# Rounding a transposed bank in two blocks of four instead of turn by turn, in a two-layer attention trunk on one Trainium2 core

## The chip, the cores and the metric

The kernel runs on one core of one Trainium2 chip. The core's engines are TensorE (PE, with its weight loads PEld), VectorE (DVE), ScalarE (ACT), GpSimd (POOL) and SyncE (SP, which issues most transfers); each works through its own list of instructions in order and waits for others by semaphores. The metric is device microseconds of one execution.

## The reference

Two layers, each `x + mixer(rms_norm(x))`, on 256 tokens of width 1024. Layer 0 is a sparse-attention mixer with 16 query heads and 4 key and value heads: compressed keys, selected blocks and a window, joined by gates. Layer 1 is a sliding-window mixer with attention sinks.

```python
def reference(x, positions, norm_gains, a_w_in, ..., b_w_in, ..., b_w_out, ...):
    for i in range(DEPTH):                      # DEPTH = 2
        h = rms_norm(x, norm_gains[i])
        y = nsa_mixer(h, ...) if i == 0 else swa_sink_mixer(h, ...)
        x = x + y
    return x

def nsa_mixer(h, ...):
    q, kc, vc, ks, vs, kw, vw, gl, z = jnp.split(h @ w_in, ...)
    ...                                         # rope, norms, three attentions, gates
    return (o.reshape(b, s, MIX_WIDTH) * jax.nn.silu(z)) @ w_out
```

## The kernel before

All arithmetic is float32. For TensorE every operand is split into a high part, rounded to the chip's fast float32 form, and a low part, the remainder; a product is three matmuls (high by high, high by low, low by high). For a weight block, a raw tile `wraw` comes by DMA (SP issues it when one of 5 raw buffers is free), ScalarE copies it to `wh` (L147; one by GpSimd in the opening), VectorE subtracts to `wl` (L175, "the weight split"). In the opening the blocks are 128x512 (two), 128x1024, 128x912 and 128x608 elements.

The 256 rows are two halves of 128. `norm_transpose` (L262 to L279) makes the transposed rows `hT` of a half, high and low: for each of two groups of four 128x128 blocks, four transposes on TensorE (L269) fill one PSUM bank `ptn`; then for each k ScalarE rounds block k times the gain to the high part (L275, "the rounding") and VectorE makes the low part from the bank and the high part (L278). There are two such banks, which serve other transposes too. A layer has four groups, so eight groups in the program; layer 0 takes the first group of both halves, some keep-warm matmuls, then the second group, and layer 1 takes the halves one after the other.

The projections of the opening of layer 0 are, in TensorE's order, `akc` (compressed keys and values, 48 matmuls of 512 columns), `avw` (window values and gates, 48 of 304), `akw` (window keys, 24 of 256), with `ptc` (16 transposes of the compressed part) among them, then `aks`. Later come `aq` (queries), `pz` (the z gate), the scores `s`, the softmax on VectorE (`cwide` L740, `p` L411), ScalarE and GpSimd, the attention `po`, and the output projections `pya`, `pyb`, which also open layer 1 (`aqb`, `akv`).

The order on each engine is not the order of the code. A scheduler with a model of times plans the whole program and places each instruction by priority (`norm_transpose` has its own offsets, 1000 in layer 0 and 200 in layer 1) and by when its inputs are due. So one edit can move rows anywhere behind it. Between instructions on different engines it sets semaphores.

Of the kernel before, what the change touches and what calls it, by code (L numbers as in the profile page):

```python
# [90 lines left out]
def tile_hybrid_trunk(ctx: ExitStack, tc: tile.TileContext, x, positions, norm_gains, a_w_in, a_cmp_pos,  # L91
# [122 lines left out]
    gT = const.tile([128, 16], F32, name="gT")  # L214
# [47 lines left out]
    def norm_transpose(xt, layer, hT, h, ns=(0, 1)):  # L262

        for n in ns:
            pt = ps_t.tile([128, 4, 128], F32, name="ptn", tag="pt")
            for k in range(4):
                nc.tensor.transpose(pt[:, k], xt[:, (4 * n + k) * 128:(4 * n + k + 1) * 128], ident)  # L269
            for k in range(4):  # L270
                kk = 4 * n + k
                gk = gT[:, 8 * layer + kk:8 * layer + kk + 1]
                hi = hT[:, 0, kk, h * 128:(h + 1) * 128]
                if GE[kk % len(GE)] == 'a':
                    nc.scalar.activation(hi, pt[:, k], AF.Copy, scale=gk)  # L275
                else:
                    nc.vector.tensor_scalar(hi, pt[:, k], gk, None, op0=ALU.mult)
                nc.vector.scalar_tensor_tensor(hT[:, 1, kk, h * 128:(h + 1) * 128], pt[:, k], gk, hi.bitcast(F32),  # L278
                                               op0=ALU.mult, op1=ALU.subtract)  # L279

# [211 lines left out]
    hT = work.tile([128, 2, 8, T], F32R, name="hT", tag="hT", bufs=1)  # L492
# [5 lines left out]
    with tc.high_priority(offset=1000):  # L498
        for n in range(2):
            for h in range(2):  # L500
                norm_transpose(xh[h], 0, hT, h, (n,))
                if n == 0 and h == 1:
                    keep_warm(NWARM2)
# [293 lines left out]
    hT = work.tile([128, 2, 8, T], F32R, name="hT1", tag="hT", bufs=1)  # L797
    with tc.high_priority(offset=200):
        for h in range(2):
            norm_transpose(xh[h], 1, hT, h)  # L800
# [107 lines left out]
```

## Time and profile before

| what | value |
|---|---|
| time, median of 3 runs | 289.93 us (288.51 to 290.54) |
| profiled execution | 287.7 us |
| its span, first to last instruction | 285.8 us |
| TensorE busy | 272.5 us, 95% |
| VectorE busy | 210.8 us, 74% |
| ScalarE busy | 194.8 us, 68% |
| GpSimd busy | 129.8 us, 45% |
| granted TensorE clock | 1.00 |

The span leaves 1.9 us of the profiled execution outside. "Busy" sums the time of an engine's instructions; the chain that ended last lies on TensorE for 75% of the span, on VectorE for 9%, on ScalarE for 6%.

### The profile page before, as it was taken

To read this page: it belongs to the slowest core of one execution; us is meant where nothing else is said; L and a number is where in the kernel's file an instruction comes from. 1 tells how busy PE (TensorE), PEld (TensorE's weight loads), DVE (VectorE), ACT (ScalarE), POOL (GpSimd) and SP (SyncE) were. 2 spreads that over 40 slices of the span, in tenths; PEclk is the share of its full clock that TensorE was granted. 3 is DMA by queue.
4 is the path that set the end of the run, shared out by engine and by line. 5 is a ranking of instruction groups with operands and counts; after the bars stand their busy time and mean duration, and the time that the engine had idled before them with its cause. 6 is when DMAs were issued, how large, how long until landed. Compare 5 with 4: busy or idle time off the path is not lost.

```text
span 285.8 us, 5305 instructions
## 1 busy us (share of the span) xinstructions
PE 272.5 (95%) x1780; PEld 228.7 (80%) x1780; DVE 210.8 (74%) x554; ACT 194.8 (68%) x466; POOL 129.8 (45%) x204
## 2 busy tenths in 40 slices
PE   6999999999999997888999999999999999999994
PEld 5857988887988996567767877779988999777774
DVE  3797757759876999857887456388987999986433
ACT  4982885577775857798979367178666787895510
POOL 8893325474630488465353320041495495513200
PEclk9999999999999999999999999999999999999999
DMA  7986955546465365200202427043696453000003
GB/s 227 337 242 229 361 155 144 145 144 172 124 160 168 116 204 165 76 0 0 77 1 73 150 74 221 0 146 85 197 292 169 145 163 133 1 2 0 0 2 147
DMA packets 33402, 37.51 MB, mean 131 GB/s; under 512 B 1968, under 2 KB 21856, under 8 KB 33248
## 3 DMA queue, kind: packets, MB, share of 16 engines
q1 hardware_dynamic: 32960, 37.16, 42.9%
q8 instruction: 14, 0.23, 0.3%
q14 instruction: 12, 0.10, 0.1%
q10 hardware_dynamic: 416, 0.02, 0.1%
HBM read 36.13 MB, written 1.05 MB: 130 GB/s over the span
## 4 chain that ended last, share of the span: by engine, by line
PE 75%; DVE 9%; ACT 6%; POOL 4%; issue 3%; DMA 1%; SPq 0%; ACTq 0%
PE pz L114 8%; PE po L114 8%; PE aqb L114 8%; PE pya L114 8%; PE aq L114 7%; PE pyb L114 6%; PE ptp L444 5%; PE aks L114 4%; PE s L114 3%; PE avw L114 2%; PE sb L114 2%; DVE wl L175 2%; PE akv L114 2%; ACT wh L147 2%; PE pza L114 2%
## 5 line engine op out<-in xcount | busy, mean ns | idle before, releaser
L175 DVE TENSOR_TENSOR wl<-wraw,wh 128x1024 fp32r<-128x1024 f32 (+2 forms) x64 | 81.7, 1281 | 25.0 <-ACT wh L147 24.9
L147 ACT ACTIVATE wh<-wraw 128x1024 fp32r<-128x1024 f32 (+3 forms) x63 | 65.0, 1033 | 29.7 <-PE pya L114 9.7
L71 POOL TENSOR_SCALAR p<-p,rg 128x128 f32<-128x128 f32 (+1 forms) x64 | 27.6, 451 | 26.8 <-DVE rg L767 9.1
L114 PE MATMUL pz<-hT,wh 128*128 128x256 f32 x192 | 36.6, 286 | 0.0
L413 ACT ACTIVATE p<-p,nm 128x128 f32<-128x128 f32 (+1 forms) x64 | 28.5, 448 | 5.7 <-DVE nm L411 5.5
L66 POOL TENSOR_TENSOR rt<-rt,rt 128x512 f32<-128x512 f32 (+2 forms) x14 | 19.1, 1375 | 28.3 <-DVE rt L319 16.7
L114 PEld LDWEIGHTS pz<-hT,wh 128*128 128x128 f32 x192 | 30.5, 191 | 0.3 <-DVE kt L699 0.2
L114 PE MATMUL pz<-hT,wl 128*128 128x256 f32 x96 | 27.4, 285 | 0.0
L411 DVE CUSTOM_DVE_ANT_0 p<-s,mask,nrq 128x128 f32<-128x128 f32 (+1 forms) x64 | 24.5, 409 | 2.3 <-PE ptp L444 2.2
L147 ACT ACTIVATE ptsb<-ptp 128x512 f32<-128x512 f32 x36 | 20.6, 590 | 6.0 <-PE ptp L444 5.9
L114 PE MATMUL s<-kt,qT 128*128 128x272 f32 (+1 forms) x96 | 19.7, 307 | 1.6 <-DVE cwide L740 1.4
L114 PE MATMUL aqb<-wh,hT 128*128 128x512 f32 x64 | 21.0, 397 | 0.0
L114 PE MATMUL aq<-wh,hT 128*128 128x512 f32 x64 | 20.6, 393 | 0.0
L71 POOL TENSOR_SCALAR pb<-pb,rg 128x128 f32<-128x128 f32 (+1 forms) x24 | 11.9, 515 | 16.7 <-DVE rg L864 13.4
L444 PE MATMUL ptp<-identr,p 128*128 128x128 f32 x96 | 16.3, 279 | 2.4 <-ACT ptsb L147 1.3
L114 PEld LDWEIGHTS pz<-hT,wl 128*128 128x128 f32 x96 | 18.3, 191 | 0.0
L114 PEld LDWEIGHTS s<-kt,qT 128*128 128x128 f32 x96 | 14.5, 189 | 3.4 <-PE s L114 1.2
L444 PEld LDWEIGHTS ptp<-identr,p 128*128 128x128 f32 x96 | 11.3, 140 | 5.5 <-ACT ptsb L147 2.0
L413 ACT ACTIVATE pb<-pb,nm 128x128 f32<-128x128 f32 (+1 forms) x32 | 14.2, 447 | 1.3 <-DVE nm L411 1.2
L275 ACT ACTIVATE hT<-ptn,gT 128x128 fp32r<-128x128 f32 x32 | 10.9, 363 | 5.8 <-DVE hT L278 3.4
L411 DVE CUSTOM_DVE_ANT_0 pb<-sb,mask,nsink 128x128 f32<-128x128 f32 (+1 forms) x32 | 13.8, 471 | 0.8 <-PE sb L114 0.6
L114 PEld LDWEIGHTS aq<-wh,hT 128*128 128x128 f32 x64 | 11.9, 188 | 2.2
(249 smaller groups left out, 727.5 us busy)
## 6 DMA issues: line engine op xcount, KB each, us to landing
wraw<-in_a_w_in_dram SPq DMA_DIRECT2D x25, 512.0 KB, 4.3
wraw<-in_b_w_in_dram SPq DMA_DIRECT2D x18, 512.0 KB, 4.0
wraw<-in_a_w_out_dram SPq DMA_DIRECT2D x8, 512.0 KB, 3.6
wraw<-in_b_w_out_dram SPq DMA_DIRECT2D x8, 512.0 KB, 3.6
x<-in_x_dram SPq DMA_DIRECT2D x4, 256.0 KB, 4.1
w<-in_cmp_w_dram SPq DMA_DIRECT2D x1, 1024.0 KB, 4.8
x<-in_x_dram SPq DMA_DIRECT2D x2, 512.0 KB, 3.7
wraw<-in_a_w_in_dram SPq DMA_DIRECT2D x2, 456.0 KB, 5.2
```

Of the source, the lines that this page charges most:

```text
L66: self.eng.tensor_tensor(out, a, b, op=op)
L71: self.eng.tensor_scalar(out, a, s0, s1, op0=op0, op1=op1)
L114: nc.tensor.matmul(o, lhsT=l, rhs=r, start=start, stop=stop)
L147: nc.scalar.activation(dst, src, AF.Copy)
L175: e_.tensor_tensor(wl[:, ks], raw[:, ks], wh[:, ks].bitcast(F32), op=ALU.subtract)
L275: nc.scalar.activation(hi, pt[:, k], AF.Copy, scale=gk)
L411: nc.vector.tensor_tensor_reduce(out=p, in0=s, in1=mk, scale=nr, scalar=floor, op0=ALU.add, op1=ALU.min, accum_out=nm)
L413: nc.scalar.activation(p, p, AF.Exp, scale=-1.0, bias=nm, accum_out=total)
L444: nc.tensor.transpose(pt[:, i], s, ident)
```

## The change

The loop over the four blocks of a bank is cut in two. All four roundings are written first, then all four low parts. Nothing is added or taken away.

```diff
                     nc.scalar.activation(hi, pt[:, k], AF.Copy, scale=gk)
                 else:
                     nc.vector.tensor_scalar(hi, pt[:, k], gk, None, op0=ALU.mult)
+
+            for k in range(4):
+                kk = 4 * n + k
+                gk = gT[:, 8 * layer + kk:8 * layer + kk + 1]
+                hi = hT[:, 0, kk, h * 128:(h + 1) * 128]
                 nc.vector.scalar_tensor_tensor(hT[:, 1, kk, h * 128:(h + 1) * 128], pt[:, k], gk, hi.bitcast(F32),
                                                op0=ALU.mult, op1=ALU.subtract)
```

The low part is on L283 after the change, and lines behind it are 5 further down. Before, ScalarE's rounding of a block waits for the low part of the block before it and each low part for its rounding. After, only the first rounding of a bank waits, and the first low part waits for the fourth rounding. ScalarE's order changes in the same way as VectorE's below: four roundings in a row, then the weights' high parts. SP's order is the same. The scheduler places rows anew on the other engines through most of the program.

VectorE, from the third bank of layer 0 to the split of the first avw weights (`wl` 128x912), before:

```order
L278 SCALAR_TENSOR_TENSOR hT<-ptn,gT,hT 128x128 x2
L175 TENSOR_TENSOR wl<-wraw,wh 128x1024
L278 SCALAR_TENSOR_TENSOR hT<-ptn,gT,hT 128x128
L175 TENSOR_TENSOR wl<-wraw,wh 128x1024
L278 SCALAR_TENSOR_TENSOR hT<-ptn,gT,hT 128x128
L517 TENSOR_SCALAR r0h<-r_129 128x2
L554 TENSOR_SCALAR trig_194<-trig,r_129 128x96 x2
L278 SCALAR_TENSOR_TENSOR hT<-ptn,gT,hT 128x128
L175 TENSOR_TENSOR wl<-wraw,wh 128x1024
L278 SCALAR_TENSOR_TENSOR hT<-ptn,gT,hT 128x128
L175 TENSOR_TENSOR wl<-wraw,wh 128x1024
L278 SCALAR_TENSOR_TENSOR hT<-ptn,gT,hT 128x128
```

The same place after:

```order
L283 SCALAR_TENSOR_TENSOR hT<-ptn,gT,hT 128x128 x4
L175 TENSOR_TENSOR wl<-wraw,wh 128x1024
L283 SCALAR_TENSOR_TENSOR hT<-ptn,gT,hT 128x128 x4
L522 TENSOR_SCALAR r0h<-r_129 128x2
L559 TENSOR_SCALAR trig_194<-trig,r_129 128x96 x2
L175 TENSOR_TENSOR wl<-wraw,wh 128x1024
L608 COPY ktv_211<-pp 128x16
L175 TENSOR_TENSOR wl<-wraw,wh 128x1024 x2
L608 COPY ktv_212<-pp 128x16
L175 TENSOR_TENSOR wl<-wraw,wh 128x912
```

The low parts, spread mostly singly between weight splits before, now stand in fours ahead of the later splits; the two small copies have moved ahead of the 912 split.

TensorE, where avw (both accumulators, 479 and 480) begins, before:

```order
L114 MATMUL akc_215<-wl,hT 128x512
L114 MATMUL akc_216<-wh,hT 128x512
L114 MATMUL avw_479<-wh,hT 128x304
L114 MATMUL avw_480<-wh,hT 128x304
L114 MATMUL akc_216<-wh,hT 128x512
L114 MATMUL akc_216<-wl,hT 128x512
L114 MATMUL akc_215<-wh,hT 128x512 x2
L114 MATMUL akc_215<-wl,hT 128x512
L114 MATMUL avw_479<-wl,hT 128x304
```

After:

```order
L114 MATMUL akc_216<-wl,hT 128x512
L114 MATMUL akc_216<-wh,hT 128x512 x2
L114 MATMUL akc_216<-wl,hT 128x512
L114 MATMUL akc_216<-wh,hT 128x512
L114 MATMUL avw_479<-wh,hT 128x304
L114 MATMUL avw_480<-wh,hT 128x304
L114 MATMUL avw_479<-wl,hT 128x304
```

Before, avw and the last akc matmuls alternate, with the last akc far into avw; after, all 48 akc matmuls stand ahead of the first avw.

TensorE, at the first scores of the second query group (`s1_1097`) among the z matmuls (`pz_1333`), before, with the numbers of the tiles:

```order
L114 MATMUL pz_1333<-hT_128,wl_1337 128x256
L114 MATMUL pz_1333<-hT_128,wh_1336 128x256 x2
L114 MATMUL s1_1097<-kt_198,qT1_205 128x272 x2
L114 MATMUL pz_1333<-hT_128,wl_1337 128x256
L114 MATMUL pz_1333<-hT_128,wh_1336 128x256 x2
```

After:

```order
L114 MATMUL pz_1333<-hT_128,wl_1367 128x256
L114 MATMUL pz_1333<-hT_128,wh_1366 128x256 x2
L114 MATMUL s1_1097<-kt_198,qT1_205 128x272 x2
L114 MATMUL pz_1333<-hT_128,wl_1367 128x256
L114 MATMUL pz_1333<-hT_128,wh_1366 128x256 x2
L114 MATMUL pz_1333<-hT_128,wl_1367 128x256
```

Before, 20 matmuls of `pz_1333` stand ahead of these scores, all with the first weight block (1336); after, 44 do, most of the second block (1366) among them. In layer 1 the first scores (`sb_2670`) stand behind 30 z matmuls instead of 17.

## Rows read from the trace of the kernel before

**Rows 1.** The page, busy time, share of the span and instructions of each engine.

```profile
PE 272.5 (95%) x1780; PEld 228.7 (80%) x1780; DVE 210.8 (74%) x554; ACT 194.8 (68%) x466; POOL 129.8 (45%) x204
```

**Rows 2.** Windows: stretch in us; its length; busy us by engine; PEclk; DMA; GB/s.

```profile
8.60:31.60 23.00, 21.92 (x108) 16.70 (x108) 19.13 (x35) 15.25 (x30) 15.94 (x23) 1.00 0.86 271
31.60:110.00 78.40, 78.02 (x550) 69.95 (x550) 60.05 (x120) 56.27 (x108) 38.17 (x34) 1.00 0.56 168
110.00:175.00 65.00, 60.45 (x391) 46.35 (x390) 45.67 (x200) 48.77 (x150) 27.60 (x65) 1.00 0.23 70
...
240.00:286.00 46.00, 41.39 (x269) 32.66 (x267) 28.45 (x87) 24.36 (x73) 9.88 (x20) 1.00 0.07 25
```

**Rows 3.** The low part's line, L278: who waited for it (us, times).

```profile
  ACT hT L275: 3.4, 8
  PEld akc L114: 2.4, 4
  PE akc L114: 0.8, 2
```

**Rows 4.** ScalarE's timeline: start us, duration us, engine, line, operation, count, idle before.

```profile
6.44 0.37 ACT L275 ACTIVATE hT<-ptn,gT 128x128 fp32r<-128x128 f32 x1 [1.35 <-PE ptn L269]
6.71 0.62 ACT L147 ACTIVATE wh<-wraw 128x512 fp32r<-128x512 f32 x1
...
8.87 1.05 ACT L147 ACTIVATE wh<-wraw 128x1024 fp32r<-128x1024 f32 x1
...
10.07 0.63 ACT L512 ACTIVATE x<-x 128x512 f32<-128x512 f32 x1
...
11.67 1.28 ACT L549 ACT_TABLE_LOAD   x1
```

**Rows 5.** VectorE's timeline in the opening.

```profile
7.36 0.69 DVE L175 TENSOR_TENSOR wl<-wraw,wh 128x512 fp32r<-128x512 f32 x1 [0.17 <-ACT wh L147]
7.97 0.60 DVE L278 SCALAR_TENSOR_TENSOR hT<-ptn,gT,hT 128x128 fp32r<-128x128 f32 x2
...
13.78 2.14 DVE L175 TENSOR_TENSOR wl<-wraw,wh 128x1024 fp32r<-128x1024 f32 x1
...
16.11 1.21 DVE L175 TENSOR_TENSOR wl<-wraw,wh 128x1024 fp32r<-128x1024 f32 x1
...
17.57 0.72 DVE L554 TENSOR_SCALAR trig<-trig,r 128x96 f32<-128x96 f32 x2
...
18.48 1.53 DVE L175 TENSOR_TENSOR wl<-wraw,wh 128x1024 fp32r<-128x1024 f32 x1
...
20.20 1.49 DVE L175 TENSOR_TENSOR wl<-wraw,wh 128x1024 fp32r<-128x1024 f32 x1
...
21.88 1.37 DVE L175 TENSOR_TENSOR wl<-wraw,wh 128x912 fp32r<-128x912 f32 x1
```

**Rows 6.** GpSimd's timeline: the last of the rope tables.

```profile
22.24 1.60 POOL L559 TENSOR_TENSOR tabs<-sm,trig 128x256 f32<-128x256 f32 x1
```

**Rows 7.** TensorE's timeline in the opening.

```profile
8.62 1.20 PE L114 MATMUL akc<-wh,hT 128*128 128x512 f32 x2
...
28.67 0.41 PE L114 MATMUL avw<-wh,hT 128*128 128x304 f32 x1
...
31.71 0.28 PE L114 MATMUL akw<-wh,hT 128*128 128x256 f32 x1
...
33.38 1.03 PE L615 MATMUL ptc<-identr,kd 128*128 128x128 f32 x8
34.17 0.48 PE L114 MATMUL akw<-wh,hT 128*128 128x256 f32 x2
...
35.45 0.40 PE L114 MATMUL aks<-wh,hT 128*128 128x512 f32 x1
```

**Rows 8.** Timelines of VectorE and TensorE in layer 1.

```profile
180.26 0.41 DVE L423 TENSOR_TENSOR oz<-of,oz 128x256 fp32r<-128x256 f32 x1
...
181.41 0.39 PE L114 MATMUL pya<-wh,oz 128*128 128x512 f32 x1
```

## The prediction, made before the changed kernel ran

> **What bounds the kernel now.** I read the page's busy shares first, then the windows by stage, then the line of the low part with who waited for it, and last the three engines' timelines of the first 36 us. TensorE is busy 272.5 of 285.8 us [rows 1], so a gain exists only where it stands idle. The windows [rows 2] say where: from 31.6 to 110 us it works 78.02 of 78.40 us, a wall in which nothing can be won but through which a lead is carried; in the opening, 8.6 to 31.6 us, it is idle 23.00 - 21.92 = 1.08 us; from 110 to 175 us 4.55 us, from 240 us to the end 4.61 us. The granted clock is 1.00 in each of them.
>
> The line of the low part [rows 3] says what the turn-by-turn order costs. ScalarE waited 3.4 us in 8 places for a low part before its next rounding; TensorE waited 2.4 + 0.8 = 3.2 us (weight loads and matmuls together), every time in akc, the first projection of layer 0. No other work of TensorE waited for a low part. So layer 1 holds no wait of TensorE that the change can remove. The 3.2 us of waits are more than the 1.08 us of idle time, since a late weight load is partly covered by the matmul running before it.
>
> **Part by part: the opening.** The change adds and removes no instruction; it makes four roundings of a bank (ScalarE) and four low parts (VectorE) two blocks. What follows is the scheduler's new order around them, and the forecast is the new place of TensorE after it. I take a state that both orders pass: akc 48 matmuls done, avw 46, akw 24 and the transposes ptc 16.
>
> *Before* reaches it thus [rows 7]: the first aks matmul starts at 35.45; akc, avw (48) and akw are done, but only 8 ptc. Eight ptc took 34.17 - 33.38 = 0.79, two avw take 2 x 0.145 = 0.29 (21 avw start between 28.67 and 31.71, 0.145 each). 35.45 + 0.79 - 0.29 = 35.95 us.
>
> *After*, ScalarE starts at 6.44 as before. Neighbours overlap: the next start is about 0.1 before the end of the one before (6.44 + 0.37 against 6.71) [rows 4]. Four roundings: 3 x 0.27 + 0.37 = 1.18, to 7.62. VectorE's four low parts, 0.26 apart (two took 0.60 [rows 5]), run 7.65 to 8.75. The first weight split of 512 (0.69) so ends at 9.3 instead of 7.36 + 0.69 = 8.05. Second bank: roundings 8.0 to 9.2, low parts to 10.3, split to 10.9, the 1024 split to 12.0. ScalarE meanwhile makes a wh of 512 and of 1024 (1.05) and two squares (about 0.63 each), so the third bank's roundings run 11.7 to 12.9, the table load (1.28, 11.67 before) 12.8 to 14.1, the fourth bank 14.3 to 15.45. VectorE: third low parts 12.9 to 13.95, the next weight split from 13.9.
>
> From here VectorE's splits set the end, and their price is not one number. The cheapest 1024 split took 1.21 us (16.11), the three others beside GpSimd's tables 1.49 to 2.14 [rows 5]. I price each by the row nearest in time: the split at 13.9 as the one at 13.78 (2.14), to 16.0; fourth low parts to 17.05; the two trig products (0.72) with the tiny r0h ahead, 0.75, to 17.8; then 1.53 (18.48), 1.53 again and 1.49 (20.20), each less the 0.07 of overlap, and two short copies of 0.1: 17.8 + 3 x 1.45 + 0.2 = 22.35; then the first 912 split as at 21.88 (1.37). It ends at **23.75**. Before, this split stood earlier in the row, between single low parts, and ended at 21.88 + 1.37 = 23.25.
>
> TensorE: akc's 48 start at 8.62 as before, because the keep-warm matmuls ahead of them do not change. Twice as wide as akw (0.119 each, below), one takes 0.24, all of them 11.4; eight transposes take 0.8, and with the first split's lateness the end lies at about 21.3, where akc's own last split (19.3) is long done. The waits for low parts are gone. In their place comes one new wait: avw now stands wholly behind akc and waits for the first 912 split, from 21.3 to 23.8. Behind it on TensorE stands everything else. From 23.80 the state takes 44 avw x 0.145 + 24 akw x 0.119 (14 of them from 31.71 to 33.38) + 16 ptc (2 x 0.79) = 6.38 + 2.86 + 1.58 = 10.82, so 34.62. Gain 35.95 - 34.62 = **1.3 us**.
>
> Bounds of this term: with every split at the 1.21 price the 912 split ends at 22.0 and the gain is 3.1; with every split at 2.14 (912 in proportion, 1.9) it ends at 26.1 and 1.0 us is lost. The gain ends when the split ends at 35.95 - 10.82 - 0.05 = 25.1. I take the middle, since the tables run until 22.24 + 1.60 = 23.84 [rows 6] and, with the table load 1.1 us later, a little longer.
>
> **Layer 1.** No wait on TensorE [rows 3], so nothing to win. What could be lost: oz and of (the gated attention of the second row half) now stand behind all eight low parts instead of six. Before, the last of the three ended at 180.26 + 0.41 = 180.67, and the matmul that reads it started at 181.41 [rows 8]. Two more low parts ahead are 2 x 0.26 = 0.52, which fits the 0.74 of slack, and the low parts take no turns with ScalarE any more. I take 0; bounds: 0 below, 0.5 above, if the cover of TensorE's aqb matmuls there were gone.
>
> **Transfers.** The same loads stand in the same order on SP. A load goes when a raw buffer comes free, with the weight split: the first split lies 1.25 us later, the one at 13.9 as before. Their readers come later too. I take 0.
>
> **Sum.** 287.7 (the profiled run) - 1.3 = 286.4. That run lies 2.2 under the median of the three runs, 289.93; on the median's scale the forecast is 289.93 - 1.3 = **288.6 us**. The wall after 31.6 us carries the lead to 110 us; behind it I assume the same idle time as before.
>
> **The rivals**, on the median's scale.
>
> *R1, the lead grows.* The whole program is planned anew, and 9.2 us of idle time lie behind the wall [rows 2]. If the new order gives back a quarter (2.3), the time is 289.93 - 1.3 - 2.3 = 286.3. For: VectorE starts ropes and sums of the queries earlier. Against: nothing in the change aims at these stages.
>
> *R2, VectorE's splits stay slow.* All at 2.14: 289.93 + 1.0 = 290.9. For: the slow rows lie beside GpSimd's tables. Against: the split at 16.11 took 1.21 [rows 5] with the tables under way until 23.84 [rows 6]. It decides from a first 912 split later than 25.1. The Trainium skill, "SBUF — State Buffer", section "Who interferes with whom", says that VectorE and GpSimd share a port pair under an exclusive lock, which would make the 2.14 the normal price there. The row at 16.11 shows it is not paid each time.
>
> *R3, slower: scores too late.* In the new order the first scores of the second query group, s1_1097, stand behind 44 z matmuls instead of 20, and in layer 1 the first scores behind 30 instead of 17. A z matmul is as wide as akw, 0.119 each: 24 x 0.119 = 2.9 and 13 x 0.119 = 1.6. If the softmax chain of the 110 to 175 us stage hangs on them fully, the time is 289.93 - 1.3 + 2.9 + 1.6 = 293.1; with layer 0 alone 291.5. For: that stage already idles 4.55 us. Against: before it VectorE has other work that the plan moved ahead. It decides when the delay exceeds the 1.3 of lead.
>
> *R4, a coarser grain.* The first split of weights ends 1.25 us later (9.3 for 8.05), because it stands behind four low parts and not one. If that delay runs through the whole opening, it takes back the 1.3: 289.9. For: what stands on VectorE is served in order. Against: TensorE does not start akc before 8.62 [rows 7], and the next splits are late by less. [...]
>
> **How the numbers follow.** A measurement of this kernel tells about 1%, 2.9 us, from no change: faster is below 287.0, slower above 292.8. Forecast 0.45 (own range 286.8 to 290.9, from the split prices; 0.05 of it under 287.0), R1 0.22 (0.19 under 287.0), R2 0.07 (with late scores 0.01 above 292.8), R3 0.20 (0.16 above 292.8, since a late score usually moves more than itself), R4 0.06. Faster 0.24, slower 0.17, same 0.59. Range: down to R1 with the cheaper splits by half, 285.4; up to R3 at its full price, 293.0. About 1 in 10 is left out on each side.
>
> **What would show it.** Right: no wait of akc for a low part; one wait of avw of 2 to 3 us for the first 912 split, which ends at 23 to 24.5; the first aks matmuls about 1.3 us earlier for the same work done; 31 to 110 us still full; layer 1's pya without a wait for oz. Wrong: a 912 split after 25.1 (R2); more than 4.55 us idle between 110 and 175 us, ended by VectorE's cwide or p (R3); or less there and behind 240 us (R1).

## The result

The changed kernel took 286.12 us (median of 4 runs, 285.36 to 286.77) and the kernel before 289.34 us beside it (288.51 to 290.54): a ratio of 0.989, with a 95% interval of 0.9855 to 0.9924. A second comparison gave 0.9902 (0.9868 to 0.9936). The gain is about 1%, or 3 us. One run of the kernel before, of 304.76 us at a mean clock of 0.855, is left out of every comparison. The profiled execution took 285.62 us, against 287.7 before, and its span is 283.8 us, against 285.8.

The page's busy times, which answer to [rows 1]:

```profile
PE 270.9 (95%) x1780; PEld 230.1 (81%) x1780; DVE 208.0 (73%) x554; ACT 194.2 (68%) x466; POOL 128.3 (45%) x204
```

The windows of the kernel after, as in [rows 2] (length, busy us of PE, PEld, DVE, ACT and POOL, PEclk, DMA share, GB/s):

```profile
8.60:31.60 23.00, 21.05 (x119) 17.89 (x118) 19.95 (x37) 16.18 (x33) 17.24 (x24) 1.00 0.81 264
31.60:110.00 78.40, 78.12 (x546) 70.07 (x544) 59.35 (x120) 56.34 (x105) 36.92 (x36) 1.00 0.60 174
110.00:175.00 65.00, 61.32 (x393) 47.62 (x395) 45.82 (x198) 49.74 (x157) 27.79 (x62) 0.97 0.24 73
```

The low part's line, now L283, with who waited for it, as in [rows 3]:

```profile
  PEld pp L607: 0.4, 1
```

No akc matmul waits for a low part any more; one small weight load waits 0.4 us. ScalarE's 3.4 us of waits are gone too. The opening window has not become fuller for it: TensorE's busy time there is 21.05 us, 0.87 less than before, because a new wait stands in it. VectorE's timeline in the opening, as in [rows 5]:

```profile
14.23 1.24 DVE L175 TENSOR_TENSOR wl<-wraw,wh 128x1024 fp32r<-128x1024 f32 x1
...
16.84 1.31 DVE L522 TENSOR_SCALAR r0h<-r 128x2 f32<-128x2 f32 x1
...
18.42 1.21 DVE L175 TENSOR_TENSOR wl<-wraw,wh 128x1024 fp32r<-128x1024 f32 x1
...
19.64 3.36 DVE L175 TENSOR_TENSOR wl<-wraw,wh 128x1024 fp32r<-128x1024 f32 x2
...
23.00 1.54 DVE L175 TENSOR_TENSOR wl<-wraw,wh 128x912 fp32r<-128x912 f32 x1
```

TensorE's timeline, as in [rows 7], from the first akc to the state of the prediction's sum:

```profile
8.92 1.20 PE L114 MATMUL akc<-wh,hT 128*128 128x512 f32 x2
...
22.21 0.44 PE L114 MATMUL avw<-wh,hT 128*128 128x304 f32 x2
24.60 0.41 PE L114 MATMUL avw<-wl,hT 128*128 128x304 f32 x1 [1.95 <-DVE wl L175]
...
35.03 0.60 PE L620 MATMUL ptc<-identr,kd 128*128 128x128 f32 x4
35.38 0.36 PE L114 MATMUL akw<-wh,hT 128*128 128x256 f32 x1
```

VectorE's weight splits (L175) run until the first 912 split ends at 23.00 + 1.54 = 24.54 us, and avw's first low-part matmul starts at 24.60 after an idle wait of 1.95 us. The state of the prediction's sum (akc 48, avw 46, akw 24, ptc 16) is reached at 35.38, against 35.95 before: a lead of 0.57 us, not 1.3. (In all there are 48 akw matmuls, not 24; in both orders the first 24 of them stand ahead of this state, so the comparison is of the same work.)

The rest of the 2.0 us lies elsewhere. Two more places in the program are the same in both orders and can be set beside each other: the first transposes of layer 1 (ptn), and the end.

| | before | after | lead |
|---|---|---|---|
| state in the opening | 35.95 | 35.38 | 0.57 |
| first ptn of layer 1 | 174.94 | 173.27 | 1.67 |
| end of the span | 285.8 | 283.8 | 2.0 |

The two ptn rows, before and after:

```profile
174.94 0.60 PE L269 MATMUL ptn<-identr,x 128*128 128x128 f32 x4
```

```profile
173.27 0.60 PE L269 MATMUL ptn<-identr,x 128*128 128x128 f32 x4
```

Between the opening and layer 1 the lead grows by 1.10 us, in layer 1 by 0.33. The first of these two is found near 70 us. Before, 16 transposes of the selected keys (ptk) stand in one piece (TensorE, start, duration, count):

```profile
69.49 0.70 PE L380 MATMUL ptk<-identr,kp 128*128 128x128 f32 x6
...
70.30 0.36 PE L380 MATMUL ptk<-identr,kp 128*128 128x128 f32 x2
71.02 1.04 PE L380 MATMUL ptk<-identr,kp 128*128 128x128 f32 x8 [0.35 <-ACT kt L381]
72.08 0.50 PE L114 MATMUL pz<-hT,wh 128*128 128x256 f32 x2
```

They share two PSUM banks with ScalarE's copies out of them, and a group of four has to wait until a bank has been copied. The waits of that stretch before the change:

```profile
PEld ptk L380 <- ACT kt L381: 0.5, 1, 0.5
...
PE ptk L380 <- ACT kt L381: 0.4, 1, 0.4
...
PEld pz L114 <- DVE kt L699: 0.2, 1, 0.2
```

After the change the new plan puts the groups apart, among the z matmuls:

```profile
69.52 0.28 PE L114 MATMUL pz<-hT,wl 128*128 128x256 f32 x1
69.64 0.45 PE L385 MATMUL ptk<-identr,kp 128*128 128x128 f32 x4
69.94 0.35 PE L114 MATMUL pz<-hT,wh 128*128 128x256 f32 x1
70.12 0.46 PE L385 MATMUL ptk<-identr,kp 128*128 128x128 f32 x4
```

Four ptk take 69.94 - 69.64 = 0.30 us there; the other eight follow at 73.61. Before, the piece from 69.49 to 72.08 took 2.59 us for 16 ptk and one ptkc (another small transpose, about 0.2): 16 at that pace are 1.2, so that about 1.2 us went in waiting, enough for the 1.10.

The stage of the scores and the softmax is as long as before. Its window in the kernel before, up to the first ptn of layer 1, with 475 matmuls and 474 weight loads:

```profile
100.00:175.00 75.00, 70.45 (x475) 56.35 (x474) 55.46 (x221) 55.08 (x163) 36.51 (x71) 1.00 0.29 88
```

The window of the kernel after with the same 475 and 474, up to its first ptn:

```profile
98.33:173.27 74.94, 71.29 (x475) 57.39 (x474) 56.36 (x226) 56.14 (x168) 36.09 (x71) 0.98 0.28 88
```

75.00 us before, 74.94 after. The granted clock (the column before the last two) is not the same in it. From 110 to 120 us, before and after:

```profile
110.00:120.00 10.00, 7.47 (x48) 5.48 (x46) 8.56 (x41) 7.92 (x29) 4.52 (x10) 1.00 0.39 113
```

```profile
110.00:120.00 10.00, 8.02 (x44) 5.88 (x44) 8.84 (x42) 7.55 (x30) 7.37 (x13) 0.83 0.24 76
```

After the change the clock stands at 0.50 for part of this stretch, TensorE is busy longer with fewer matmuls, and the stage is as long all the same. The clock fell between 111 and 120 us in all seven profiles with 44 z matmuls ahead of the scores of the second query group, the changed kernel's two among them, and in none of the three with 20 or 31 (before, layer 1 alone, avw first on the kernel before). No run tests whether that order is the cause.

### The profile page after: what moved, and what is told of

Read it like the earlier page. It is cut to its first block, busy times and chain, and to the rows that moved or that the text cites. A ratio compares the mean times of both kernels' runs of the same rounds, so it can differ in the third digit from the quotient of the medians.

```text
span 283.8 us, 5308 instructions
## 1 busy us (share of the span) xinstructions
PE 270.9 (95%) x1780; PEld 230.1 (81%) x1780; DVE 208.0 (73%) x554; ACT 194.2 (68%) x466; POOL 128.3 (45%) x204
## 3 DMA queue, kind: packets, MB, share of 16 engines
HBM read 36.13 MB, written 1.05 MB: 131 GB/s over the span
## 4 chain that ended last, share of the span: by engine, by line
PE 84%; ACT 5%; DVE 4%; issue 2%; POOL 1%; DMA 1%; SPq 0%; DVEq 0%; ACTq 0%
PE pz L114 11%; PE po L114 8%; PE pya L114 8%; PE aq L114 8%; PE aqb L114 8%; PE pyb L114 6%; PE ptp L449 5%; PE s L114 4%; PE pza L114 4%; PE aks L114 4%; PE sb L114 2%; PE avw L114 2%; PE akv L114 2%; PE akw L114 2%; PE ph L114 2%
## 5 line engine op out<-in xcount | busy, mean ns | idle before, releaser
L175 DVE TENSOR_TENSOR wl<-wraw,wh 128x1024 fp32r<-128x1024 f32 (+2 forms) x64 | 79.6, 1253 | 21.5 <-ACT wh L147 21.4
L66 POOL TENSOR_TENSOR rt<-rt,rt 128x512 f32<-128x512 f32 (+2 forms) x14 | 20.6, 1477 | 34.1 <-DVE rt L324 34.1
L431 DVE SCALAR_TENSOR_TENSOR of<-po,zt 128x256 f32<-128x256 f32 x14 | 5.9, 423 | 11.5 <-PE po L114 11.4
```

The costliest lines, as they stand in the source:

```text
L66: self.eng.tensor_tensor(out, a, b, op=op)
L175: e_.tensor_tensor(wl[:, ks], raw[:, ks], wh[:, ks].bitcast(F32), op=ALU.subtract)
L431: nc.vector.scalar_tensor_tensor(of, po, 0.5, zt[:, 2 * g4:2 * g4 + 2, h * 128:(h + 1) * 128], op0=ALU.mult, op1=ALU.mult)
```

## The experiments

Each ratio is to the kernel before, run beside it.

**Layer 0 alone.**

```diff
+                if not (layer == 0):
+                    nc.vector.scalar_tensor_tensor(hT[:, 1, kk, h * 128:(h + 1) * 128], pt[:, k], gk, hi.bitcast(F32),
+                                                   op0=ALU.mult, op1=ALU.subtract)
...
-            for k in range(4):
+            for k in range(4 if (layer == 0) else 0):
```

> The roundings and low parts of a bank stand in two blocks in layer 0 only; layer 1 goes turn by turn as before. Theory (the gain lies in layer 0: 0.6 us in the opening, about 1.0 us where four groups of ptk transposes no longer stand back to back near 70 us, the rest between 75 and 110 us): the span is 1.7 us shorter than before (285.8), 284.1, and the time about 1.7 to 3 us under that of before. Rival (a good part of the gain comes from layer 1): less than 1 us under before.

Measured: 287.46 us, ratio 0.9929 (0.9904 to 0.9954), 1.8 us under before by the medians (287.46 for 289.27); span 285.5. The time agrees with the theory, the span does not: 1.4 us more than the 284.1 expected. The trace says where. The avw wait was 2.06 us, much as in the changed kernel, but behind it the granted clock fell, in the windows of 2 us:

```profile
24.00:26.00 2.00, 1.73 (x11) 1.74 (x12) 2.00 (x5) 0.91 (x2) 1.85 (x2) 0.94 0.14 28
26.00:28.00 2.00, 2.00 (x9) 2.00 (x9) 2.00 (x5) 0.42 (x1) 1.17 (x2) 0.50 0.85 295
28.00:30.00 2.00, 2.00 (x14) 2.00 (x14) 1.27 (x2) 0.64 (x1) 0.00 (x0) 0.71 0.98 394
```

The same windows of the changed kernel's first profile:

```profile
24.00:26.00 2.00, 1.40 (x10) 1.40 (x11) 2.00 (x4) 0.83 (x2) 1.85 (x2) 1.00 0.17 65
26.00:28.00 2.00, 2.00 (x17) 2.00 (x17) 2.00 (x4) 0.82 (x1) 1.52 (x2) 1.00 0.87 266
```

From 26 to 28 us it stood at 0.50, the lower of its two levels; in the changed kernel's first profile it stayed at 1.00. The state was reached at 36.58 instead of 35.38. From there to the first ptn of layer 1 it took 138.01 us (changed kernel 137.89, before 138.99), and from there to the end 110.9 (changed kernel 110.53, before 110.86). So layer 0 holds the 1.1 us of the ptk groups and not the 0.33 of layer 1.

**Layer 1 alone.** The same edit with the layers exchanged.

> Two blocks in layer 1 only; layer 0 turn by turn as before. Theory (TensorE waits for no low part in layer 1): the time is that of before within 0.5 us, at most the 0.3 us by which the two traces drift apart behind 190 us. Rival (layer 1 carries part of the gain): 1 us or more under before.

Measured: 288.71 us, ratio 0.9989 (0.9964 to 1.0014): not to be told from no change, as the theory had it. The trace is finer than the time. From the first ptn of layer 1 (175.92) to the end (286.5) it took 110.58 us, as in the changed kernel, and 0.28 less than before. The windows put it into the end of the program, the same 269 matmuls in 45.80 and 45.47 us. Before:

```profile
240.00:285.80 45.80, 41.39 (x269) 32.66 (x267) 28.45 (x87) 24.36 (x73) 9.88 (x20) 1.00 0.07 25
```

After the change:

```profile
238.33:283.80 45.47, 41.36 (x269) 32.63 (x267) 28.19 (x87) 24.79 (x73) 9.90 (x20) 0.99 0.07 24
```

There the kernel before has a wait of 0.5 us of the last output projection for the attention (VectorE's ozb), which is not among the waits after; a wait of 0.4 us of the scores for the softmax (nm) stands there instead. That the 0.3 us come from this exchange, a by-product of the new plan, is read from the traces and not shown by a run of its own; no transposed bank is near.

**The kernel before, with the ptk groups apart.**

```diff
-HPC, HPK, NWARM2 = 300, 250, 4
+HPC, HPK, NWARM2 = 300, 100, 4
```

> The kernel before, turn by turn in both layers, with the priority offset of the key preparation lowered from 250 to 100, so that the four groups of ptk transposes near 70 us stand apart, with z matmuls between, as after the change; the opening's order is that of before. Theory (about half of the gain is this lost wait, which the new plan removes and not the change itself): 1.0 us under before, the waits of ptk for ScalarE's copies gone, the opening's times unchanged. Rival (the gain is the opening's, carried through): no difference to before.

Measured: 287.39 us, ratio 0.9934 (0.9905 to 0.9962), 1.9 us under before, more than the 1.0 expected, with 1.1 us (0.9962) at the interval's near end. In the trace, state to first ptn took 174.61 - 36.63 = 137.98 us: the whole of the changed kernel's gain in this stretch, 1.0 us, without the change. The two waits of ptk are gone. The priority moved other rows as well: in this order, too, the scores s1_1097 stand behind 44 z matmuls, so the 1.0 us is what the whole re-planned stretch gives. Of the other 0.9 us the trace shows nothing: its opening, in the order of before, even took 0.68 longer (36.63 to 35.95), and by the spans the run is only 0.3 us shorter than the profile of before (285.5 for 285.8).

**The avw weights first**, on the changed kernel: in `keys_window` the loop that loads and multiplies the three avw blocks is written ahead of the one for akw.

```diff
+            accv = banks("avw", "s")
+            for k0, nk in ((0, 3), (3, 3), (6, 2)):
+                w = load_w(awi, k0, nk, 2304, 304)
...
             acck = banks("akw")
             for k0 in (0, 4):
                 w = load_w(awi, k0, 4, 2048, 256)
...
-            accv = banks("avw", "s")
```

> The changed kernel with the avw weights loaded and split ahead of the akw weights. In the changed kernel VectorE splits two akw blocks (3.36 us together) before the first avw block, for which TensorE waits 1.95 us. Theory (that wait sits on the path): the wait is gone or under 0.7 us, the same state of the opening is reached 1 to 1.5 us earlier, and the time is 1 to 1.5 us under the changed kernel. Rival (the wait returns at akw or ptc, or the new plan behind it gives the lead back): within 0.5 us of the changed kernel.

Measured: 284.41 us, ratio 0.9823 (0.9788 to 0.9857), 1.7 us under the changed kernel's 286.1, which was measured in another comparison. This is the fastest of the kernels that compute everything. The one wait of TensorE in the opening's view of waits:

```profile
PE ptc L620 <- ACT kd L616: 1.1, 1, 1.1
```

VectorE's timeline, the three avw splits:

```profile
19.43 4.38 DVE L175 TENSOR_TENSOR wl<-wraw,wh 128x912 fp32r<-128x912 f32 x3
```

TensorE's timeline, the start of avw's low parts and the last four ptc:

```profile
22.06 0.39 PE L114 MATMUL akc<-wh,hT 128*128 128x512 f32 x1
22.29 0.30 PE L114 MATMUL avw<-wl,hT 128*128 128x304 f32 x1
...
34.24 0.66 PE L620 MATMUL ptc<-identr,kd 128*128 128x128 f32 x4 [1.15 <-ACT kd L616]
```

The three avw splits now end at 23.81, and avw runs from 22.29 without a wait. A wait of 1.15 us has come at the last four ptc for ScalarE's kd, which takes part of the 1.95 back. The state is reached at 34.36 (akw's 25th matmul starts at 34.65 with two more avw done, 0.29), 1.0 us earlier than in the changed kernel's profile, as the theory had it; the first ptn of layer 1 starts at 172.46, 0.81 earlier. The rest of the 1.7 us is not in this trace.

**The changed kernel again.**

> The changed kernel once more, beside the other three on one chip. All theories: 1.1% under before, as in the first comparison (interval 0.8 to 1.4%). If the two halves of the change add up, its gain is that of layer 0 alone (0.71%) plus that of layer 1 alone (0.11%), 0.8%.

Measured: 286.08 us, ratio 0.9902 (0.9868 to 0.9936). The halves, 0.71% and 0.11%, sum to 0.82%, inside this interval. In this execution the clock fell as in the run with layer 0 alone. The windows:

```profile
24.00:26.00 2.00, 2.00 (x11) 2.00 (x12) 2.00 (x5) 0.69 (x1) 1.86 (x2) 0.70 0.56 75
26.00:28.00 2.00, 2.00 (x9) 2.00 (x9) 1.61 (x4) 0.41 (x1) 0.74 (x2) 0.50 0.80 332
```

TensorE's row at the end of the wait ahead of it:

```profile
23.85 0.41 PE L114 MATMUL avw<-wl,hT 128*128 128x304 f32 x1 [2.06 <-DVE wl L175]
```

Span 284.7 us, state at 36.16. The wait before the fall was 2.06 us, against 1.95 in the first profile, which kept its clock.

**Without the wide rope tables.** `tabc` and `tabs` for the first four gains are set to a constant early instead of computed by GpSimd, so this kernel leaves out work and its output is not that of the others.

```diff
-        for lo, hi, tr in ((0, 4, trig0), (4, 6, trig)):
+        for lo, hi, tr in ((4, 6, trig),):
```

> The changed kernel without GpSimd's four 256-wide rope tables (they are set to a constant early, so the keys are rotated wrongly); TensorE's order is the same. In the changed kernel r0h took 1.31 us and the two akw splits 1.68 each beside these tables. Theory (VectorE shares a way to memory with GpSimd, and the opening's new wait is that): r0h under 0.3, the splits at 1.21 to 1.25, the first 912 split ends about 2 us earlier, the avw wait falls from 1.95 to under 0.4 us, and the time is 1.5 to 2 us under the changed kernel. Rival (the splits' price has another cause): splits as slow as before and no gain.

Measured: 284.25 us, ratio 0.9826 (0.9795 to 0.9857), 1.8 us under the changed kernel beside it. VectorE's timeline, r0h, the two akw splits and the first 912 split:

```profile
16.44 1.45 DVE L522 TENSOR_SCALAR r0h<-r 128x2 f32<-128x2 f32 x1
...
19.38 2.35 DVE L175 TENSOR_TENSOR wl<-wraw,wh 128x1024 fp32r<-128x1024 f32 x2
...
21.73 1.09 DVE L175 TENSOR_TENSOR wl<-wraw,wh 128x912 fp32r<-128x912 f32 x1
```

TensorE's row after the avw wait:

```profile
22.88 0.41 PE L114 MATMUL avw<-wl,hT 128*128 128x304 f32 x1 [0.62 <-DVE wl L175]
```

The two akw splits took 2.35 us together (3.36), the 912 split 1.09 (1.54); it ended 1.7 us earlier, at 22.82; the avw wait was 0.62, where under 0.4 was expected. The theory holds for the splits. It fails for r0h (1.45): the expectation had it beside the wide tables, but in the changed kernel it ended at 16.84 + 1.31 = 18.15 us, before the first of them started (18.40). In both kernels it runs beside narrow tables, left in here; what makes it slow is not shown. The Trainium skill, "SBUF — State Buffer", section "Who interferes with whom", has VectorE and GpSimd share a port pair under an exclusive lock; the splits' 1.18 against 1.68 agree with it.

**The avw weights first on the kernel before**, the same edit as above.

> The kernel before, turn by turn, with the avw weights loaded and split ahead of akw, the counterpart of the same edit on the changed kernel. Theory (avw waited little before: 0.8 us of weight loads and matmuls together, so that the edit pays only where the blocks of four have made avw late): 0.3 to 1 us under before, most of it from ptk groups that now stand partly apart. Rival (avw first is worth the same 1.7 us with either order): 2 us or more under before.

Measured: 286.21 us, ratio 0.9897 (0.9868 to 0.9927), 3.2 us under before. The rival was right: this edit alone gives as much as the whole change. Not all of it is the order, though: all six of its runs have a mean clock of 0.998 or more, and only five of the 17 of the kernel before beside them have 0.997 or more. Against the median of these five, 288.35 us, the edit gives 2.1 us, and by the profiled spans 1.5 (284.3 for 285.8). The expectation had read the 0.8 us that avw waited before as the edit's whole worth. But the two splits that move behind avw also stood between low parts that akc waited for:

```profile
PE akc L114 <- DVE hT L278: 0.5, 1, 0.5
```

akc's matmuls now wait 0.5 us in one place for a low part. In the profile of the kernel before it was 0.8 us in 2 places [rows 3]. In the profile with the ptk groups apart, whose opening has the order of before, the same view has:

```profile
PE akc L114 <- DVE hT L278: 2.1, 3, 1.1
```

That is 2.1 us in 3 places, so the same order waits unequally long from one execution to the next, and between these profiles the edit saves 0.3 to 1.6 us of such waits.

**The second banks of layer 0 alone** (`layer == 0 and n == 1` as the condition of the first experiment).

> Two blocks only for the second bank of each row half in layer 0; the first banks and layer 1 turn by turn. The first weight split then ends early again (8.05 for 9.6 us on the trace) and the ptk groups stand apart as in the changed kernel. Theory (the lateness of the first split costs nothing, the ptk groups give about 1.2 us): as with the change in layer 0 alone, 1.5 to 2.2 us under before. Rival (the coarser grain of the first banks costs): at least 0.7 us faster than layer 0 alone, 2.7 us or more under before.

Measured: 289.14 us, ratio 1.0002 (0.998 to 1.0023): no gain, where both theory and rival had at least 1.5 us. The ptk groups stand apart here too. But the plan made other waits of TensorE, from 8 to 37 us:

```profile
PE akw L114 <- ACT kd L619: 1.9, 1, 1.9
PE akc L114 <- DVE wl L175: 0.7, 1, 0.7
```

The same view from 34 to 62 us:

```profile
PE aks L114 <- ACT gt L666: 1.3, 1, 1.3
```

akw waits 1.9 us for its PSUM banks, which ScalarE still reads for kd, and aks 1.3 us for its own, read for the gate. They stand against what the ptk groups give. What blocks of four are worth thus depends on the plan that comes out around them: with half of them it was as slow as before.

## Why the prediction was right, and where it was not

The forecast, 288.6 us or 1.3 under before, has the sign, and the measured 286.1 lies in its range (285.4 to 293.0), but near the end: it is R1's time (286.3), not that of the forecast. Counted from the 289.34 measured beside it the forecast is 288.0, and the gain of 3 us is more than twice the 1.3. Since R1's mechanism gave only 0.3 us of it, at the end, the range held in part by luck.

- *No wait of akc for a low part*: right, by the source row above. akc started at 8.92, though, not at 8.62 as before.
- *One new wait of avw, 2 to 3 us, for the first 912 split*: right in place and nearly in size, 1.95 us. The split ended at 24.54, not 23.75. Of the parts, r0h with the trig products was mis-sized (16.84 to 18.42, 1.58 us for 0.75), and so were the akw splits (1.68 each for 1.53 and 1.49) and the 912 (1.54 for 1.37); the splits at 14.23 and 18.42 were paid too much (1.24 for 2.14, 1.21 for 1.53). That the wide rope tables set the prices of the akw splits and of the 912 is shown by the run without them; r0h kept its price there. The cheap end was named as a bound (22.0), and that run came to 22.82.
- *The state at 34.62, gain 1.3 us*: this term failed in size. The lead was 0.57 in the first profile. What was mis-sized there is the end of the 912 split alone: from the end of the wait to the state the sum has 10.82 us and the trace 35.38 - 24.60 = 10.78, while the split came 0.79 late and the state 0.76. Over the profiles that share an opening, the state was reached at 35.38, 36.58 and 36.16 (changed kernel, layer 0 alone, changed kernel again) and at 35.95, 36.87 and 36.63 (before, layer 1 alone, ptk groups apart; the first aks at 36.37 and 36.13, with the same 0.50 added). The means are 36.04 and 36.48, a lead of 0.4 us, and single executions lie up to 0.7 from their mean, so these six do not fix the lead. The sum left out the clock, which makes part of this spread: it fell in the opening of two of the first three (36.58, 36.16) and of one of the others (36.87). With the clock at 1.00 there it is 35.38 against 35.95 and 36.63.
- *From 31.6 to 110 us nothing can be won, a lead is only carried*: this step failed, and it is the larger part. The wall from 31.6 to 110 us was called full because TensorE was busy 78.02 of 78.40 us. It held about 1.1 us to win all the same (the stretch from the state to layer 1 took 138.99 us before and 137.89 after, and from about 100 us to layer 1 both are equally long): the eight ptk at 71.02 count as 1.04 us of busy time, waits between them included, where two groups take 0.60 apart. The busy share does not show that; the times of two states that both orders pass do. The run with the ptk groups apart has 1.0 us of it without the change.
- *R1 (the lead grows)*: its time was right, its place wrong. It put the gain into the idle time behind the wall; 1.1 of it lies inside the wall and 0.3 in the last 46 us. Its sign, less than 4.55 us idle from 110 to 175 us, did come (65.00 - 61.32 = 3.68), but it is no gain: over the same 475 matmuls TensorE is busy 0.84 us longer, with the clock down for part of them, in a stage as long as before.
- *R3 (scores too late)*: did not happen. The stage took 74.94 us for 75.00. The run with the ptk groups apart has the scores as late, and is still 1.0 us quicker than before from the state to layer 1 (137.98 us).
- *R2 and R4*: the tables did cost, but less than R2's full price; the first split was later (9.64 in the trace), and akc's weight loads waited 0.3 us for it in the first profile of the changed kernel.
- *Layer 1, 0*: right for the low parts; the 0.33 us lie at the very end, where the plan's waits are others.

What stays open: the medians give the ptk groups 1.9 us where the trace shows 1.0, and the whole change 3 us where the traces show 2.0. Part of this lies in the profile of before (287.7): it is among the shortest of its kernel's runs (medians 289.3 and 289.4), and its clock did not fall. Of the 39 runs of the kernel before beside the experiments, 11 have a mean clock of 0.997 or more and a median of 288.35 us; the other 28 have 0.991 to 0.994 and 289.66, 1.3 us more. The changed kernel's ten runs split in the same way: five at 0.992 or 0.993 with a median of 285.56 us, five at 0.987 or 0.988 with 286.77. For the rest the intervals, 0.8 to 1.0 us to either side, leave room.

## What to carry to other kernels

Where a scheduler plans the whole program, cost an edit by what stands next in the new order and by what the plan loses elsewhere, and test the same loss alone (here the ptk groups by one priority, the avw weights by the order of two loops) before crediting the edit: by themselves these gave 1.9 and 3.2 us, the change 3 (all by the medians, the clock's part included). In a stage where TensorE's busy share is full, compare the times at which the same work is done, since waits of a third of a microsecond between weight loads hide in it. And when two stages of splits feed one engine, split first what is multiplied first: on the changed kernel that is worth another 1.7 us.

## What was not expected of the hardware

The granted clock fell in the opening in some executions and not in others of the same order. It fell to 0.50 after avw waits of 2.06 us in two runs, and stayed at 1.00 there after waits of 1.95 (the first profile) and 1.88 (second banks alone, before akw). With the order of before it fell in the run with layer 1 alone, whose waits there were 0.85 us at most:

```profile
21.00:24.00 3.00, 3.00 (x9) 1.84 (x10) 3.00 (x5) 1.53 (x3) 3.00 (x3) 0.56 0.62 175
24.00:27.00 3.00, 3.00 (x20) 3.00 (x20) 1.84 (x4) 0.56 (x2) 0.36 (x1) 0.88 0.50 145
```

and stayed at 1.00 in the run with the ptk groups apart, with waits of 2.1 us in all. So the length of a wait alone does not tell. From the first avw matmul after the wait to the state, the changed kernel took 35.38 - 24.60 = 10.78 us with the clock at 1.00 and 36.16 - 23.85 = 12.31 us with the fall: 1.5 us, more than the predicted gain. In the profiles a mean clock of 0.987 or 0.988 goes with two falls, one of them in the opening. A mean clock of 0.988 or less came in 5 of the changed kernel's 10 runs, in 8 of 10 with layer 0 alone and in 6 of 12 with the second banks alone, all with a wait of about 2 us in the opening, and in none of the 12 runs with avw first on the changed kernel or without the wide tables, whose profiles wait 1.15 and 0.62 us. That fits the wait as an occasion for the fall; it was not tested by itself.

The second surprise is the price of GpSimd's tables: a VectorE split of 1024 cost 1.68 us beside two of them and 1.18 without them, but 1.21 at 18.42 us, beside this one:

```profile
18.40 1.83 POOL L562 TENSOR_TENSOR tabc<-sm,trig 128x256 f32<-128x256 f32 x1 [0.28 <-DVE trig L559]
```

So a split beside a table does not pay each time.
